# Two order edits around a layer's norms: w_out's last weight split behind a turn, SwiGLU 1's first post-norm multiply ahead of a weight split

## The chip, the cores and the metric

One core of a Trainium2 chip runs the whole layer. The metric is the device time of one execution in microseconds (us). Five engines work side by side, each through a queue of its own: PE (TensorE, matmuls; its weight loads are shown apart as PEld), DVE (VectorE), ACT (ScalarE), POOL (GpSimd) and SP (SyncE, which only issues transfers). An instruction waits for others through semaphores. About 0.2% of the time, 1.46 us here, is what a measurement of this kernel can tell from no change.

## The reference

A decoder layer on 256 tokens of width 1024, in fp32: a SwiGLU block (hidden width 2816), a mixer with a state-space branch and an attention branch, and a second SwiGLU block. Each is wrapped in RMS norms. Cut to what the change touches:

```
h = h + 0.5 * rmsnorm(swiglu(rmsnorm(h, ffn1_pre_g), ...), ffn1_post_g)
u = rmsnorm(h, mix_pre_g)
z, xbc, dt_raw, q, k, v, gate_logits = split(u @ w_in)
...
merged = gates[:, :, 0] * y_ssd + gates[:, :, 1] * y_att
h = h + rmsnorm(merged @ w_out, mix_post_g)
h = h + 0.5 * rmsnorm(swiglu(rmsnorm(h, ffn2_pre_g), ...), ffn2_post_g)
```

## The kernel before

**Splits.** Every fp32 product is made of three faster matmuls. An operand x is split into hi, a rounded copy of x (a cast on ACT), and lo = x - hi (a subtraction on DVE, which therefore follows the cast). PE then sums hi*hi, lo*hi and hi*lo. This holds for weights and activations alike. A weight chunk of 1 MB comes by DMA into one of three `raw` buffers, and `split_steps` (L256 to L275) splits it in two halves: cast `whi`, subtraction `wlo`, each 128 x 1024. Where the second lo part is done, the raw buffer is given back and the next load is issued on SP. Most products run over the two blocks of 128 tokens (block 0, block 1) and, on the output side, over two halves of 512 columns.

**Quads.** For some weights four 256-row chunks are combined as in Strassen's and Winograd's scheme (class `Quad`): seven products of sums replace eight. `Quad.split(p)` (L127 to L139) makes the hi and lo of piece p; the sums themselves (`wt`) are formed on DVE one or two pieces ahead. For w_out the pieces come in the order 1, 2, 6, 5, 3, 7, 4 (`MIXED`), and the two plain chunks of the lower half of w_out lie between 7 and 4 in the list of units. Piece 4's sum is formed together with piece 7's, at the split of piece 3, and at that point the raw buffers of the quad are given back. Its split thus issues no transfer.

**Who sets the order.** In the stages concerned only PE's order is written out by hand (`own_order(PE)`); it runs in the order of the program text. ACT, DVE and SP are ordered by the framework's planner. It takes for each engine the first instruction in the text that is ready when the engine comes free, by estimated times, and each engine's queue is then fixed: on the chip an instruction waits in its queue for its semaphores, and what stands behind it waits too. Buffers of one pool (`k4`, 29 of 4 KB a partition, hold most hi and lo parts) are handed out in the order of the text. `behind(m, "lo")` (L237 to L240) adds an edge of pure order to a DVE instruction: the planner must not place it ahead of the instruction noted in `normed["lo"]`. Such an edge carries no semaphore.

**w_out (`mm_mixed`, from L764).** The merged activations come as blocks (half of the columns, block of tokens). Both blocks of the first half are turned (transposed on PE into `pmg`, then split into `mh`, ml by `split`, L331 to L333, called in `turn_merged`) before `mm_mixed` begins. The two of the second half are turned inside it, one behind piece 6 and one behind piece 5, by `turn_next`. Line 793, `split_to(taken[0] + 9)`, puts the splits of all nine units into the text ahead of piece 1, the last of them piece 4. PE's order is: piece 1, 2, 6, first turn (block 0), piece 5, second turn (block 1), `plain(0, 0, 0)`, which is the first work that reads the turned second half of block 0, piece 3, further plain products, piece 7, block 1's plain products, piece 4. The post-norm of block 0 follows its last plain products: an add (L1728), a multiply by the gain (L617), a sum of squares on ACT (L518), the root on POOL (L523, L524), and h (L657).

**SwiGLU 1's end (`mm_n`, from L664).** The last three chunk pairs of the down product are held: PE runs block 0's first half of columns, then its second half, then block 1's. After each half, `half` adds the parts of the quads' bank to the accumulator (L1015) and calls `norm_half` (L607 to L617): a sum of squares on ACT (`jp`), for the first half a small add `ep` on DVE (L614), and the multiply by the gain into `og` (L617). `norm_end` (L648 to L657) makes the reciprocal root on ACT (`rp`) and h on DVE. Behind the call `ready(0)` (L714) the text splits the first chunk of the weights of V, the next product; of the four V chunks, the last has its parts held behind norm instructions of block 1. V's product (`Norm.products`, tile `pn_mx`, L394) runs over the four chunks for block 0, with the chunks' lo parts last.

Of the kernel before, what the change touches and what calls it, by code (L numbers as in the profile page):

```python
# [55 lines left out]
def tile_hybrid_layer(ctx: ExitStack, tc: tile.TileContext, x, ffn1_pre_g, ffn1_w_gate, ffn1_w_up,  # L56
# [25 lines left out]
    def pj(name):  # L82

        return ps.tile([P, 512], F32, tag="pj", name=name, bufs=3)
# [149 lines left out]
    normed = {"lo": None, "cast": None}  # L234
# [7 lines left out]
    taken = [0]  # L242
# [13 lines left out]
    def split_steps():  # L256


        i, _ = units[len(splits)]
        load_to(i + 1)  # L260
        r, shape = raws[i], chunks[i][1]
        nj = shape[1] // 2
        his, los = [], []
        splits.append((his, los))
        for q in range(2):
            hi = k4([P, nj, shape[2]], f"whi{i}{q}", F32R)
            lo = k4([P, nj, shape[2]], f"wlo{i}{q}", F32R)
            his.append(hi)
            los.append(lo)
            js = slice(q * nj, (q + 1) * nj)  # L270
            last_cast[0] = behind(nc.scalar.copy(hi, r[:, js, :]), "cast").ins  # L271
            m = nc.vector.tensor_sub(lo, r[:, js, :], hi.bitcast(F32))  # L272
            last_wlo[0] = behind(m, "lo").ins
            yield
        raws[i] = None  # L275
        load_to(i + 1 + RAW_BUFS)
# [23 lines left out]
    def split_to(n):  # L300

        while len(splits) < min(n, len(units)):
            of, p = units[len(splits)]
            if p is not None:
                splits.append(of.split(p))
                continue
            for _ in split_steps():
                pass

    def ahead_of(i, n):  # L310

        n *= 4
        while n > 0 and i < len(units):
            n -= 4 if units[i][1] is None else 1
            i += 1
        return i

    def take(ahead=AHEAD):

        i = taken[0]  # L320
        taken[0] += 1
        split_to(ahead_of(i, ahead))
        (of, p), w = units[i], splits[i]
        splits[i] = None
        if p is not None:
            return w
        his, los = w
        nj = chunks[of][1][1] // 2
        return (lambda j: his[j // nj][:, j % nj, :], lambda j: los[j // nj][:, j % nj, :])
# [334 lines left out]
    def mm_n(acc, acts, ready, turned, begun=lambda: None, pairs=None, begin=True, taken_all=lambda: None, norms=None,  # L664
             half=lambda b, q: None, quarters=(), tail=None):

        pairs = pairs or range(len(acts) // 2)
        n = len(pairs)
        held = []

        def one(i, w, parts, late=True, others=True, cs=slice(0, 512), to=None):


            wh, wl = w
            for kt in range(2):  # L680
                ah, al = acts[2 * pairs[i] + kt]
                for b, qs in parts:
                    ts = slice(b * P, (b + 1) * P)
                    for x_, w_ in ((ah, wh), (al, wh), (ah, wl)):
                        if not (late if kt == 1 and w_ is wl else others):
                            continue
                        for q in qs:
                            nc.tensor.matmul(acc[b][q][:, cs] if to is None else to, x_[:, ts],  # L688
                                             w_(kt)[:, halves[q]][:, cs],
                                             start=to is not None and kt == 0 and x_ is ah and w_ is wh or  # L690
                                             begin and i == 0 and kt == 0 and x_ is ah and w_ is wh,
                                             stop=i == (n - 2 if quarters and b and q and to is None else n - 1)
                                             and kt == 1 and w_ is wl)
                if i == 0:
                    begun()

        for i in range(n):
            w = take(min(n - i, AHEAD))
            if i < n - TAIL:
                one(i, w, ((0, (0, 1)), (1, (0, 1))))  # L700
            else:
                held.append((i, w))
        taken_all()
        own_order(PE)
        for q in range(2):
            for i, w in held:

                one(i, w, ((0, (q,)),), late=not norms or q == 1 or i < n - 1)
                if norms and q == 1 and i == n - TAIL:
                    one(*held[-1], ((0, (0,)),), others=False)  # L710
                    half(0, 0)
            if not norms or q == 1:
                half(0, q)
        ready(0)  # L714
        split_to(ahead_of(taken[0], AHEAD - 2))
        if norms:
            normed["lo"] = norms[0]["h"]
        split_to(ahead_of(taken[0], AHEAD - 1))
        for q in range(2):
            for i, w in held:  # L720
                if q == 1 and i == n - TAIL + (1 if norms else 0):
                    turned()
                if quarters and q == 1 and i == n - 1:
                    for cs, to in zip(quarters, tail):
                        one(i, w, ((1, (q,)),), cs=cs, to=to)
                else:
                    one(i, w, ((1, (q,)),))
            half(1, q)
        if not norms:
            split_to(ahead_of(taken[0], AHEAD))  # L730
        ready(1)
        if norms:
            if len(splits) < len(units):
                steps = split_steps()
                normed["lo"] = norms[1]["mul"]
                next(steps)
                normed.update(lo=norms[1]["h"], cast=norms[1]["exp"])
                for _ in steps:
                    pass
            normed.update(unit_done)  # L740
# [23 lines left out]
    def mm_mixed(acts, sums, turn_next, half, done, turned):  # L764


        at = {1: "a", 6: "a", 7: "a", 4: "a", 2: "b", 5: "d", 3: "d"}
        banks = {"a": pj("acc_mxa")}
        begun = set()
        sh, sl = sums  # L770
        p1, u2, p5, c4 = (k2([P, 512], f"{n}_mx") for n in ("p1", "u2", "p5", "c4"))

        def mm(o, x_, w_, stop):
            nc.tensor.matmul(banks[o], x_, w_, start=o not in begun, stop=stop, skip_group_check=True)
            begun.add(o)

        def piece(p, w):
            o, (wh, wl) = at[p], w
            if o not in banks:
                banks[o] = bg([P, 512], f"acc_mx{o}")  # L780
            for kt in range(2):
                ah, al = of_piece(p, kt, acts[:4], sh, sl)
                for x_, w_ in ((ah, wh), (al, wh), (ah, wl)):
                    mm(o, x_, w_(kt), kt == 1 and w_ is wl and p in (1, 5, 6, 7))

        def plain(b, q, i):
            o, (wh, wl) = (("b", "d"), ("a", "e"))[b][q], ws[i]
            for kt in range(2):
                ah, al = (x_[:, b * P:(b + 1) * P] for x_ in acts[4 + 2 * i + kt])
                for x_, w_ in ((ah, wh), (al, wh), (ah, wl)):  # L790
                    mm(o, x_, w_(kt)[:, halves[q]], i == 1 and kt == 1 and w_ is wl)

        split_to(taken[0] + 9)
        piece(1, take(0))
        nc.scalar.copy(p1, banks["a"])
        piece(2, take(0))
        piece(6, take(0))
        nc.scalar.copy(u2, banks["a"])
        turn_next()
        piece(5, take(0))  # L800
        nc.scalar.copy(p5, banks["d"])
        turn_next()
        w3, w7 = take(0), take(0)
        ws = [take(0) for _ in range(2)]
        w4 = take(0)
        plain(0, 0, 0)
        piece(3, w3)
        split_to(taken[0] + 1)
        steps = split_steps()
        next(steps)  # L810
        plain(0, 1, 0)
        plain(0, 0, 1)
        half(0, 0, banks["b"], p1)
        plain(0, 1, 1)
        half(0, 1, banks["d"], u2)
        normed["lo"] = done(0)
        for _ in steps:
            pass
        piece(7, w7)
        nc.vector.tensor_tensor(c4, banks["a"], p5, ALU.add)  # L820
        banks["e"] = pj("acc_mxe")
        plain(1, 1, 0)
        plain(1, 1, 1)
        half(1, 1, banks["e"], c4)
        turned()
        piece(4, w4)
        for i in range(2):
            plain(1, 0, i)
        half(1, 0, banks["a"], None)
        normed["lo"] = done(1)  # L830
# [946 lines left out]
```

## Time and profile before

| what | us |
|---|---|
| median of 3 runs | 730.65 |
| lowest and highest | 729.85, 730.78 |
| the profiled execution's own time | 731.11 |
| its span, first to last instruction | 729.4 |
| PE busy in the span | 720.5 |
| DVE busy | 621.8 |
| ACT busy | 478.8 |

The profiled execution took 1.71 us more than its span; this lies around the span. A row of the timeline gives start, duration, engine, source line, operation and output <- inputs, and in brackets the time the engine stood idle before the row with what released it. Rows that follow each other closely are merged ("x2"). Matmuls overlap in a pipeline: one of 512 columns is shown with 0.39 us though the next starts 0.23 us after it, so a delay of PE is read from start to start. ACT and DVE rows also overlap a little: two lo parts of 1.22 us take 2.35 us together.

### The profile page before, as it was taken

Reading aid. Unit: us, or ns where it says so; the run is one execution under the profiler, and the core shown is the slowest. Engines: PE = TensorE matmul, PEld = TensorE weight load, DVE = VectorE, ACT = ScalarE, POOL = GpSimd, SP = SyncE. Lnnn points to the kernel's source line nnn. Section 1 sums busy time; section 2 is a strip of 40 time slices with the busy share of each in tenths; the row PEclk is TensorE's granted clock in tenths of the full one; section 3 lists DMA queues with packets and bytes.
Section 4 is the critical chain, followed back from the end, with each engine's and each line's share of the span. In section 5 each row is a group of like instructions: output and inputs, shape, how many; then the busy total and the mean of one; then the engine's idle time right before and its main releaser. Section 6 shows DMA issues by size and latency. Waiting matters only on the chain.

```text
span 729.4 us, 10595 instructions
## 1 busy us (share of the span) xinstructions
PE 720.5 (99%) x4019; PEld 619.4 (85%) x4019; DVE 621.8 (85%) x950; ACT 478.8 (66%) x816; POOL 30.9 (4%) x63
## 2 busy tenths in 40 slices
PE   9999999999999999999999999999999999999996
PEld 7888888888778889999888788888788888888885
DVE  6978788999979999777996998789776878789996
ACT  5667566666867676969965577784654756576562
POOL 4300000000200000000000000000011000000000
PEclk9999999999999999999999999999999999999999
DMA  8884655567573557666564664464543655754451
GB/s 298 234 263 152 220 163 184 174 230 259 181 232 118 180 167 231 215 181 212 154 224 146 205 225 135 153 234 170 181 138 116 231 182 165 231 191 156 180 194 58
DMA packets 94451, 137.93 MB, mean 189 GB/s; under 512 B 2668, under 2 KB 68800, under 8 KB 94400
## 3 DMA queue, kind: packets, MB, share of 16 engines
q1 hardware_dynamic: 91728, 129.51, 53.8%
q0 software_dynamic: 2368, 7.22, 3.2%
q8 instruction: 31, 0.51, 0.3%
q10 hardware_dynamic: 304, 0.53, 0.2%
q14 instruction: 20, 0.16, 0.1%
HBM read 136.17 MB, written 1.08 MB: 188 GB/s over the span
## 4 chain that ended last, share of the span: by engine, by line
PE 88%; DVE 5%; ACT 2%; DMA 2%; issue 2%; SPq 0%; DVEq 0%; ACTq 0%
PE pup_f L353 14%; PE pg_f L353 14%; PE pxs L353 6%; PE pws L394 6%; PE pgt L394 6%; PE acc_f2p L842 5%; PE pbc L353 3%; PE pk L353 3%; PE pq L353 3%; PE pn_f L394 3%; PE pwd L394 3%; PE pn_f L410 3%; PE pn_mx L394 2%; PE acc_f2p L688 2%; PE pz L345 2%
## 5 line engine op out<-in xcount | busy, mean ns | idle before, releaser
L272 DVE TENSOR_TENSOR wlo<-raw,whi 128x1024 fp32r<-128x1024 f32 x212 | 252.7, 1221 | 18.7 <-ACT whi L271 18.2
L271 ACT CAST whi<-raw 128x1024 fp32r<-128x1024 f32 x212 | 214.4, 1048 | 14.0 <-DMA raw<-in_w_in_dram 5.8
L353 PE MATMUL pg_f<-u_f,whi 128*128 128x512 f32 x288 | 69.1, 390 | 0.0
L353 PE MATMUL pup_f<-u_f,whi 128*128 128x512 f32 x288 | 68.7, 391 | 0.0
L353 PEld LDWEIGHTS pg_f<-u_f,whi 128*128 128x128 f32 x288 | 53.9, 188 | 11.2
L353 PEld LDWEIGHTS pup_f<-u_f,whi 128*128 128x128 f32 x288 | 52.9, 188 | 10.2
L131 ACT CAST wqh<-wt 128x1024 fp32r<-128x1024 f32 x24 | 25.2, 1054 | 23.3 <-DVE wt L123 21.9
L353 PEld LDWEIGHTS pg_f<-u_f,wlo 128*128 128x128 f32 x288 | 36.9, 191 | 1.4
L353 PE MATMUL pup_f<-u_f,wlo 128*128 128x256 f32 x288 | 37.5, 283 | 0.0
L353 PE MATMUL pg_f<-u_f,wlo 128*128 128x256 f32 x288 | 37.4, 283 | 0.0
L359 ACT COPY su_f<-pup_f 128x256 f32<-128x256 f32 x36 | 13.2, 372 | 35.9 <-PE pup_f L353 35.9
L353 PEld LDWEIGHTS pup_f<-u_f,wlo 128*128 128x128 f32 x288 | 35.9, 192 | 0.0
L360 DVE TENSOR_TENSOR su_f<-pup_f,su_f 128x256 f32<-128x256 f32 x36 | 15.2, 422 | 24.0 <-ACT su_f L359 23.9
L394 PE MATMUL pgt<-whi,u_mx 128*128 128x512 f32 x128 | 33.1, 393 | 0.0
L343 PE MATMUL pz<-u_mx,whi 128*128 128x256 f32 x128 | 31.6, 284 | 0.0
L342 PE MATMUL pz<-u_mx,whi 128*128 128x256 f32 x128 | 31.6, 284 | 0.0
L353 PE MATMUL pxs<-u_mx,whi 128*128 128x512 f32 x128 | 29.9, 390 | 0.0
L137 DVE TENSOR_TENSOR wql<-wt,wqh 128x1024 fp32r<-128x1024 f32 x24 | 29.1, 1220 | 0.2
L137 DVE TENSOR_TENSOR wql<-raw,wqh 128x1024 fp32r<-128x1024 f32 x21 | 25.5, 1220 | 3.4 <-ACT wqh L131 3.4
L394 PEld LDWEIGHTS pgt<-whi,u_mx 128*128 128x128 f32 x128 | 23.6, 188 | 5.3 <-issue 0.7
L353 PEld LDWEIGHTS pxs<-u_mx,whi 128*128 128x128 f32 x128 | 23.8, 188 | 4.8
L332 ACT CAST gh_f<-sg_f 128x512 fp32r<-128x512 f32 x18 | 11.2, 621 | 23.2 <-DVE sg_f L995 20.3
(487 smaller groups left out, 1607.5 us busy)
## 6 DMA issues: line engine op xcount, KB each, us to landing
raw<-in_w_in_dram SPq DMA_DIRECT2D x40, 1024.0 KB, 5.2
raw<-in_ffn_w_down_dram SPq DMA_DIRECT2D x22, 1024.0 KB, 4.8
raw<-in_ffn_w_gate_dram SPq DMA_DIRECT2D x20, 1024.0 KB, 5.5
raw<-in_ffn_w_up_dram SPq DMA_DIRECT2D x20, 1024.0 KB, 5.2
raw<-in_ssd_w_branch_dram SPq DMA_DIRECT2D x8, 1024.0 KB, 4.9
acb<-acd POOLq DMA_DIRECT2D x8, 512.0 KB, 4.4
raw<-in_da_w_branch_dram SPq DMA_DIRECT2D x4, 1024.0 KB, 5.0
raw<-in_w_out_dram SPq DMA_DIRECT2D x4, 1024.0 KB, 6.2
```

The costliest lines, as they stand in the source:

```text
L131: nc.scalar.copy(hi, src)
L137: nc.vector.tensor_sub(lo, src, hi.bitcast(F32))
L271: last_cast[0] = behind(nc.scalar.copy(hi, r[:, js, :]), "cast").ins
L272: m = nc.vector.tensor_sub(lo, r[:, js, :], hi.bitcast(F32))
L342: nc.tensor.matmul(acc[m], wh(j)[:, cs], ah(k0 + j), start=first and j == ks[0], stop=False)
L343: nc.tensor.matmul(acc[m], wh(j)[:, cs], al(k0 + j), start=False, stop=False)
L345: nc.tensor.matmul(acc[m], wl(j)[:, cs], ah(k0 + j), start=False, stop=last and j == ks[-1])
L353: nc.tensor.matmul(to, w_(j)[:, m * P:(m + 1) * P], x_(j), start=first and j == 0, stop=not first and j == KD - 1, skip_group_check=True)
L360: nc.vector.tensor_tensor(dst, acc[:, :T], dst, ALU.add)
L394: nc.tensor.matmul(acc, a(k0 + j), b(j), start=first and i == 0, stop=last and i == 11)
L410: nc.tensor.matmul(accs[b], x_(k0 + j), w_(j), start=first and j == 0 and w_ is wh and x_ is acts[b][0], stop=last and j == 3 and w_ is wl)
L842: nc.tensor.matmul(bank[p], x_, w_, start=p not in begun, stop=last and p in (1, 5, 6, 7))
```

## The change

Three lines change. In `mm_n` the multiply of block 0's first half is noted as the instruction behind which "lo" instructions must stay: this holds for the lo parts of V's first chunk (up to L715, the next unit) and for the adds of `half(0, 1)`. `mm_n` serves both SwiGLU blocks. In `mm_mixed` the list is split up to the second plain chunk only (eight units), and the ninth, piece 4, is split behind the first `turn_next()`.

```diff
@@ -709,6 +709,7 @@
                 if norms and q == 1 and i == n - TAIL:
                     one(*held[-1], ((0, (0,)),), others=False)
                     half(0, 0)
+                    normed["lo"] = norms[0]["mul"]
             if not norms or q == 1:
                 half(0, q)
         ready(0)
@@ -790,13 +791,14 @@
-        split_to(taken[0] + 9)
+        split_to(taken[0] + 8)
         piece(1, take(0))
         nc.scalar.copy(p1, banks["a"])
         piece(2, take(0))
         piece(6, take(0))
         nc.scalar.copy(u2, banks["a"])
         turn_next()
+        split_to(taken[0] + 6)
         piece(5, take(0))
         nc.scalar.copy(p5, banks["d"])
         turn_next()
```

## The prediction

> **What bounds the kernel now.** I read the page first (engines, chain), then the waits of PE, then the timelines of PE, ACT and DVE around those waits.
>
> ```profile
> PE 720.5 (99%) x4019; PEld 619.4 (85%) x4019; DVE 621.8 (85%) x950; ACT 478.8 (66%) x816; POOL 30.9 (4%) x63
> ...
> PE 88%; DVE 5%; ACT 2%; DMA 2%; issue 2%; SPq 0%; DVEq 0%; ACTq 0%
> ```
> ```profile
> PE acc_mxb L774 <- DVE ml L333: 0.9, 1, 0.9
> PE pn_mx L394 <- DVE wlo L272: 0.5, 1, 0.5
> ```
>
> PE is the bound: it is busy all but 8.9 us, and the chain of waits lies on it for 88%. Nothing can be won but PE's own stalls. Behind the start its waits show just the two above: in w_out for a turned activation, in V for a weight's lo part. Each edit stands ahead of one of them on DVE. PE in w_out, some rows left out:
>
> ```profile
> 523.99 0.60 PE L1689 MATMUL pmg<-ident,gt 128*128 128x128 f32 x4
> 524.35 0.48 PE L774 MATMUL acc_mxd<-wqh,sh 128*128 128x512 f32 x1
> ...
> 525.13 0.40 PE L774 MATMUL acc_mxd<-wqh,sh 128*128 128x512 f32 x1
> ...
> 525.82 0.60 PE L1689 MATMUL pmg<-ident,gt 128*128 128x128 f32 x4
> 526.26 0.50 PE L774 MATMUL acc_mxb<-whi,mh 128*128 128x512 f32 x1
> 527.64 0.50 PE L774 MATMUL acc_mxb<-whi,ml 128*128 128x512 f32 x1 [0.88 <-DVE ml L333]
> ...
> 528.21 0.40 PE L774 MATMUL acc_mxb<-whi,mh 128*128 128x512 f32 x1
> ```
>
> The wait costs more than its 0.88 us, because the bracket starts where the pipelined matmul before it ends. Start to start is the honest measure. From the first turn to the fourth matmul behind it: 525.13 - 523.99 = 1.14. From the second turn: 528.21 - 525.82 = 2.39. The same work, so the stall is **1.25 us**.
>
> A rule to weigh against the bracket: the Trainium skill ("Trainium Kernel Development and Optimization", Performance Expectations) calls matmul busy time a bad measure of how far a kernel is from its limit, because matmuls are pipelined, and names the busy share of the weight loads instead. Two windows of 10 us (PE, then PEld, DVE, ACT, POOL, clock, DMA):
>
> ```profile
> 520.00:530.00 10.00, 9.12 (x44) 7.28 (x43) 9.56 (x13) 7.35 (x11) 0.00 (x0) 1.00 0.65 209
> 530.00:540.00 10.00, 10.00 (x49) 8.34 (x49) 7.84 (x11) 4.42 (x10) 0.88 (x2) 1.00 0.33 107
> ```
>
> Loads fall from 8.34 to 7.28, which is 10 x 1.06 / 8.34 = 1.27 us of lost time. Matmul busy would give 0.88. The rule's reading and start to start agree; with 0.88 the sum below would be 0.37 smaller.
>
> **Part one, w_out.** Why ml is late, ACT first, then DVE:
>
> ```profile
> 524.67 1.05 ACT L131 CAST wqh<-wt_mx 128x1024 fp32r<-128x1024 f32 x1
> 525.62 0.59 ACT L332 CAST mh<-pmg 128x512 fp32r<-128x512 f32 x1
> ```
> ```profile
> 522.96 2.36 DVE L272 TENSOR_TENSOR wlo<-raw,whi 128x1024 fp32r<-128x1024 f32 x2
> 525.76 1.23 DVE L137 TENSOR_TENSOR wql<-wt_mx,wqh 128x1024 fp32r<-128x1024 f32 x1 [0.44 <-ACT wqh L131]
> 526.90 1.28 DVE L333 TENSOR_TENSOR ml<-pmg,mh 128x512 fp32r<-128x512 f32 x2
> 528.16 3.50 DVE L272 TENSOR_TENSOR wlo<-raw,whi 128x1024 fp32r<-128x1024 f32 x3
> 533.19 0.69 DVE L1728 TENSOR_TENSOR p_mx<-acc_mxb,p_mx 128x512 f32<-128x512 f32 x1 [1.53 <-PE acc_mxb L774]
> ```
>
> Piece 4's cast and subtraction stand ahead of the first turn's on both engines, though the piece is the last that PE reads. The change moves two instructions, no transfer: the quad's raw buffers were given back earlier. With them behind the turn, the turn's transposes end at 523.99 + 0.60 = 524.59 and mh takes wqh's place at 524.67, until 525.26. DVE ends its lo parts at 525.32; ml of block 0 runs from about 525.35 to 526.05 (half of the merged pair, some 0.69). PE wants mh at 526.18 (0.36 behind 525.82, as at the first turn) and ml one matmul later, not before 526.4. Both are there, ml with 0.3 to spare, so all 1.25 is gained.
>
> What is queued behind: wqh next on ACT, 525.2 to 526.2, and then the copy of piece 5's product and mh of block 1, within 0.1 of where they are. wql on DVE ends at about 527.5, ml of block 1 at 528.1, the lo parts of SwiGLU 2 follow at 528.1 as before. Block 1 and piece 4 are read after 534, so this cost lies under PE's work. DVE's cover is thinner than it was. It is free at 528.1 + 3.50 = 531.6, and p_mx's add, 1.25 earlier, falls due at 531.94: 0.3 spare where 1.53 stood. The four pool buffers only change partners. I take 1.25. Bounds: 0 if the planner leaves the order as it was, 1.25 at most since the stall then is gone.
>
> **Part two, SwiGLU 1.** PE in V:
>
> ```profile
> 194.80 0.61 PE L394 MATMUL pn_mx<-wlo,u_mx 128*128 128x512 f32 x2
> 195.87 0.72 PE L394 MATMUL pn_mx<-wlo,u_mx 128*128 128x512 f32 x2 [0.46 <-DVE wlo L272]
> 196.44 1.09 PE L394 MATMUL pn_mx<-whi,u_mx 128*128 128x512 f32 x4
> ```
>
> Four matmuls took 196.44 - 194.80 = 1.64 us. A row of four lasts 1.09 and a row of two 0.61, so a step is 0.24 and four are 0.96: a stall of **0.68**. The awaited lo part started at 194.60 and DVE worked with hardly a gap from 179.44 on. DVE, then ACT:
>
> ```profile
> 177.30 0.68 DVE L1015 TENSOR_TENSOR p_f<-acc_f1p,p_f 128x512 f32<-128x512 f32 x1
> 179.44 1.23 DVE L272 TENSOR_TENSOR wlo<-raw,whi 128x1024 fp32r<-128x1024 f32 x1 [1.46 <-ACT whi L271]
> 180.59 0.69 DVE L617 TENSOR_TENSOR og_f<-p_f,pg_f 128x512 f32<-128x512 f32 x1
> 181.19 0.14 DVE L614 TENSOR_SCALAR ep_f<-sp_f 128x1 f32<-128x1 f32 x1
> 181.25 0.68 DVE L1015 TENSOR_TENSOR u_f<-acc_f1p,u_f 128x512 f32<-128x512 f32 x1
> ...
> 183.59 1.41 DVE L657 SCALAR_TENSOR_TENSOR h<-og_f,rp_f,h 128x512 f32<-128x512 f32 x2
> 194.60 1.21 DVE L272 TENSOR_TENSOR wlo<-raw,whi 128x1024 fp32r<-128x1024 f32 x1
> ```
> ```profile
> 178.36 2.00 ACT L271 CAST whi<-raw 128x1024 fp32r<-128x1024 f32 x2 [5.82 <-DMA raw<-in_w_in_dram]
> 180.26 0.62 ACT L518 ACTIVATE jp_f<-p_f 128x512 f32<-128x512 f32 x1
> 180.79 0.19 ACT L518 ACTIVATION_READ_ACCUMULATOR jp_f<-p_f 128x1 f32 x1
> ...
> 181.97 0.63 ACT L518 ACTIVATE jp_f<-u_f 128x512 f32<-128x512 f32 x1
> ...
> 183.05 0.20 ACT L427 ACTIVATE rp_f<-rp_f 128x1 f32<-128x1 f32 x1
> ```
>
> At 177.98 DVE took V's lo part, whose chunk had not landed, and idled 1.46 with the multiply ready behind it. Ahead of the lo part the multiply fits into that gap (178.0 to 178.7), and its 0.60 (181.19 - 180.59) falls off DVE's row. How much reaches V depends on ACT. **(a)** ACT keeps its order: ep needs the read at 180.98, so the add starts at 181.07 instead of 181.25: 0.18. **(b)** Casts and lo parts alternate in the pool's order of buffers, so V's second cast can be placed only once its first lo part is; that is now later in the plan, and the square jp of p_f, ready since 177.98, goes ahead of it. Then jp runs at 179.31 to 180.03, the second cast ends at 181.08, and the two have changed places, so what follows on ACT stays put. The add starts at 180.64, the second lo part at 181.24, the second multiply ends near 183.0, and h waits for rp at 183.25: 183.28 instead of 183.59, 0.31. **(c)** All 0.60, or the stall's 0.68, if the later square moves up too. From h on the row is dense and PE gets the same shift at 195.87. Against it: the add is barred by the same edge and could be placed ahead of the lo part with the square still late; then DVE idles until 181.0, h comes about 1.0 late and V with it. So the bounds are -1.0 and +0.68.
>
> Whether casts and lo parts alternate shows on ACT in w_out, at the second plain chunk's second cast:
>
> ```profile
> 521.47 0.59 ACT L795 COPY p_mx<-acc_mxa 128x512 f32<-128x512 f32 x1 [1.76 <-PE acc_mxa L774]
> 521.95 1.05 ACT L271 CAST whi<-raw 128x1024 fp32r<-128x1024 f32 x1
> ```
>
> It comes behind the copy, though ACT idled 1.76 ahead of that with the chunk long loaded; the chunk's first lo part is the one at 522.96 on DVE, late behind the merge. So the alternation holds there, and I take (b), **0.31**.
>
> In SwiGLU 2 the new edge costs nothing: no splits are left, and the add there stands behind the multiply already, waiting for PE. If that cover were gone, the edge still carries no semaphore.
>
> **Sum.** 1.25 + 0.31 = 1.56. The profiled execution took 731.11 (span 729.4 and 1.71 around it): 729.55 after. The median of the runs lies 0.46 below it: 730.65 - 1.56 = **729.1**.
>
> **Rivals.**
> - *Only w_out pays*: ACT's order holds, or PE meets V's lo part as late as before: 1.25 to 1.43, 729.3. For it: the swap on ACT in (b) is the planner's choice by its own times, which no row shows. Against it: the multiply leaves DVE's full row in any case.
> - *V's stall goes whole*: 1.25 + 0.68: 728.7. It needs the square of u_f ahead of a cast, which the order of before has behind it.
> - *Given back in w_out's norm*: one more lo part (1.17, a third of 3.50) ahead of p_mx's add makes it 0.9 late, h and the turn behind it too: 730.0. For it: 0.3 spare. Against it: that part's cast is fourth and must come first.
> - *The edit in w_out changes nothing*, the planner putting piece 4 first again since it is ready: 730.3. Against it: mh's buffers come first in the text.
> - *Slower*: the planner's order tips over far from the edits, in the state-space branch. There ACT's exponentials E feed PE without slack:
>
> ```profile
> 293.73 2.00 ACT L271 CAST whi<-raw 128x1024 fp32r<-128x1024 f32 x2
> ...
> 303.98 0.96 DVE L1360 TENSOR_TENSOR E<-E,cbm 128x768 f32<-128x768 f32 x1 [0.73 <-ACT E L427]
> ```
> ```profile
> 304.99 2.82 PE L1370 MATMUL py<-E,X 128*64 128x256 f32 x32
> ```
>
> PE's py starts 0.05 behind the last E. Two more casts ahead of it cost 2.00 for each of the four groups in which it happens; one group gives 731.1, two give 733.1, and from one on the gain is gone. For it: ACT's order is re-planned behind the first edit. Against it: PE bounds that stretch, so everything there moves together.
>
> **How the numbers follow.** Forecast 0.52, w_out alone 0.14, whole stall 0.13, given back 0.07, no change in w_out 0.05, slower 0.09. What can be told from no change is 0.2%, 1.46 us: faster means below 729.19. The forecast lies 0.1 below that line, so with a scatter of some 0.35 between runs 0.33 of its 0.52 counts as faster, with 0.13 of the whole stall and 0.04 of w_out alone: 0.50. Slower by 0.2% is the last case, 0.09; the rest, 0.41, is within. The range, 728.3 to 730.6, takes the cases from 728.7 to 730.3 with 0.3 to 0.4 for scatter and leaves out the slower case. The forecast's own is 728.7 to 729.5.
>
> **What would show it.** Right: no wait of PE for ml; mh ahead of the cast of piece 4 on ACT; from the second turn to the fourth matmul 1.14; the multiply og_f before 179; jp of p_f before V's second cast; PE's wait in V shorter by 0.3, not gone. Wrong: a wait of PE at the turn behind w_out, DVE reaching p_mx's add with no idle time before it, py waiting longer for E, or h of block 0 later against the add of p_f than now (6.29).

## The result, and the profile after

| | before | after |
|---|---|---|
| median on the same chip, 22 runs each (us) | 730.26 | 728.78 |
| lowest and highest | 729.40, 730.88 | 728.42, 730.06 |
| the profiled execution's own time | 731.11 | 728.73 |
| its span | 729.4 | 727.0 |

The ratio is 0.9982 [0.9975, 0.9988]: 1.3 us gained, with an interval of 0.9 to 1.8. The medians differ by 1.48. The 1.46 us that a measurement of this kernel can tell from no change lies between the two: the interval is clear of zero, and the gain about as large as that line. The forecast was 729.1, its own range 728.7 to 729.5.

The page of the changed kernel, engines and chain of waits:

```profile
PE 719.0 (99%) x4019; PEld 618.8 (85%) x4019; DVE 621.4 (85%) x950; ACT 479.0 (66%) x816; POOL 32.2 (4%) x63
...
PE 96%; ACT 2%; DMA 1%; DVE 1%; issue 0%; SPq 0%; DVEq 0%; ACTq 0%
```

The waits of PE (engine, tile and line, what it waited for: us in all, times, longest):

```profile
PE warm L487 <- DVE zeros L467: 1.1, 1, 1.1
PE pn_f L410 <- DVE whi L289: 0.7, 1, 0.7
```

Both waits for DVE that stood in w_out and V are gone; what is left lies at the kernel's start. The chain lies on PE for 96% instead of 88%, but that says little of the change: a second profile of the kernel before, further down, has 96% too.

w_out on PE, first turn, the fourth matmul behind it, second turn, and the matmuls behind that:

```profile
522.89 0.60 PE L1691 MATMUL pmg<-ident,gt 128*128 128x128 f32 x4
...
524.03 0.40 PE L775 MATMUL acc_mxd<-wqh,sh 128*128 128x512 f32 x1
...
524.72 0.60 PE L1691 MATMUL pmg<-ident,gt 128*128 128x128 f32 x4
525.07 0.48 PE L775 MATMUL acc_mxb<-whi,mh 128*128 128x512 f32 x1
525.39 0.39 PE L775 MATMUL acc_mxb<-whi,ml 128*128 128x512 f32 x1
525.62 0.40 PE L775 MATMUL acc_mxb<-wlo,mh 128*128 128x512 f32 x1
525.86 0.39 PE L775 MATMUL acc_mxb<-whi,mh 128*128 128x512 f32 x1
```

From the second turn to the fourth matmul it is 525.86 - 524.72 = 1.14, as behind the first (524.03 - 522.89). Before it was 2.39: the 1.25 us is gained to the hundredth. The profiles of the experiments below agree: the stretch takes 2.38 to 2.41 in all six with w_out's old order, that of before among them, and 1.13 to 1.14 in all eight with the new one. ACT and DVE show how:

```profile
523.57 0.59 ACT L332 CAST mh<-pmg 128x512 fp32r<-128x512 f32 x1
524.05 1.06 ACT L131 CAST wqh<-wt_mx 128x1024 fp32r<-128x1024 f32 x1
```
```profile
524.20 0.69 DVE L333 TENSOR_TENSOR ml<-pmg,mh 128x512 fp32r<-128x512 f32 x1
525.14 1.23 DVE L137 TENSOR_TENSOR wql<-wt_mx,wqh 128x1024 fp32r<-128x1024 f32 x1 [0.25 <-ACT wqh L131]
...
530.83 0.69 DVE L1730 TENSOR_TENSOR p_mx<-acc_mxb,p_mx 128x512 f32<-128x512 f32 x1 [0.26 <-PE acc_mxb L775]
```

The cast mh stands ahead of piece 4's cast wqh, ml runs at 524.20, and piece 4's subtraction comes behind it. The idle time ahead of p_mx's add shrinks from 1.53 to 0.26.

The Trainium skill ("Trainium Kernel Development and Optimization", Performance Expectations) would have the weight loads' busy share watched instead of the matmuls'. The 10 us that hold w_out's turns show it (PE, PEld, DVE, ACT, POOL, clock, DMA): 8.29 us of loads where 7.28 stood, so the rule reads this gain where matmul busy, 9.12 and then 10.00, shows 0.88 of it.

```profile
518.90:528.90 10.00, 10.00 (x50) 8.29 (x49) 9.64 (x13) 7.35 (x11) 0.00 (x0) 1.00 0.66 211
```

SwiGLU 1's end, DVE and then ACT:

```profile
177.10 0.68 DVE L1017 TENSOR_TENSOR p_f<-acc_f1p,p_f 128x512 f32<-128x512 f32 x1
177.82 0.69 DVE L617 TENSOR_TENSOR og_f<-p_f,pg_f 128x512 f32<-128x512 f32 x1
178.58 1.23 DVE L272 TENSOR_TENSOR wlo<-raw,whi 128x1024 fp32r<-128x1024 f32 x1
179.72 0.14 DVE L614 TENSOR_SCALAR ep_f<-sp_f 128x1 f32<-128x1 f32 x1
179.79 0.68 DVE L1017 TENSOR_TENSOR u_f<-acc_f1p,u_f 128x512 f32<-128x512 f32 x1
...
182.41 1.41 DVE L657 SCALAR_TENSOR_TENSOR h<-og_f,rp_f,h 128x512 f32<-128x512 f32 x2 [0.21 <-ACT rp_f L427]
```
```profile
177.50 1.05 ACT L271 CAST whi<-raw 128x1024 fp32r<-128x1024 f32 x1 [5.01 <-DMA raw<-in_w_in_dram]
178.45 0.62 ACT L518 ACTIVATE jp_f<-p_f 128x512 f32<-128x512 f32 x1
...
179.07 2.12 ACT L271 CAST whi<-raw 128x1024 fp32r<-128x1024 f32 x2
...
182.17 0.20 ACT L427 ACTIVATE rp_f<-rp_f 128x1 f32<-128x1 f32 x1
```

The multiply og_f stands ahead of V's first lo part, the square jp of p_f ahead of V's second cast, and h waits for rp. From V's first cast to h it is 182.41 - 177.50 = 4.91, where the kernel before has 183.59 - 178.36 = 5.23: 0.32 less, with 0.31 forecast. But PE in V does not wait at all:

```profile
194.52 1.07 PE L394 MATMUL pn_mx<-wlo,u_mx 128*128 128x512 f32 x4
195.43 1.07 PE L394 MATMUL pn_mx<-whi,u_mx 128*128 128x512 f32 x4
196.34 1.03 PE L532 MATMUL pu_mx<-ident,un_mx 128*128 128x128 f32 x8
```

Four lo matmuls take 195.43 - 194.52 = 0.91 from start to start. The 1.64 of before therefore held a stall of 0.73, and all of it is gone, not 0.3 of it. More than the edit is at work. V's first cast began 8.08 behind the issue of its load before (170.28 to 178.36) and 7.42 behind it after (170.08 to 177.50):

```profile
170.28 4.91 SPq L253 DMA_DIRECT2D raw<-in_w_in_dram  x3
```
```profile
170.08 11.91 SPq L253 DMA_DIRECT2D raw<-in_w_in_dram  x4
```

The chunk landed 0.66 sooner behind its issue, and the change touches neither this load nor one ahead of it. Whether the stall went by the change or by chance was left to the experiments.

The lead of the execution after over that before grows from 0.20 at that issue to 1.03 at the turn behind V's first block (197.37 and 196.34), 1.10 at w_out's first turn, 2.35 at w_out's fourth matmul (528.21 and 525.86) and 2.37 at the last h. So 1.25 came in w_out, 0.83 between V's load and V's end, and 0.2 was there before any edit acts. SwiGLU 2, which the new edge also serves, lost nothing: from w_out's fourth matmul to the last h it is 196.82 before and 196.80 after.

### The profile page after: what moved, and what is told of

Same layout as the page of the kernel before. It is cut to its first block, busy times and chain, and to the rows that moved or that the text cites. A ratio compares the mean times of both kernels' runs of the same rounds, so it can differ in the third digit from the quotient of the medians.

```text
span 727.0 us, 10595 instructions
## 1 busy us (share of the span) xinstructions
PE 719.0 (99%) x4019; PEld 618.8 (85%) x4019; DVE 621.4 (85%) x950; ACT 479.0 (66%) x816; POOL 32.2 (4%) x63
## 4 chain that ended last, share of the span: by engine, by line
PE 96%; ACT 2%; DMA 1%; DVE 1%; issue 0%; SPq 0%; DVEq 0%; ACTq 0%
PE pup_f L353 14%; PE pg_f L353 14%; PE pxs L353 6%; PE pws L394 6%; PE pgt L394 6%; PE acc_f2p L844 5%; PE acc_f1p L844 5%; PE pbc L353 3%; PE pk L353 3%; PE pq L353 3%; PE pn_mx L394 3%; PE pn_f L394 3%; PE pwd L394 3%; PE pn_f L410 3%; PE acc_f1p L688 2%; PE acc_f2p L688 2%
```

## The experiments

The runs of the kernel before have their median at 729.92, 729.93, 729.98 and 729.69 in the four groups that follow.

**Each edit alone.** Only the two lines in `mm_mixed`, and only the line in `mm_n`:

```diff
# wout_only
-        split_to(taken[0] + 9)
+        split_to(taken[0] + 8)
...
         turn_next()
+        split_to(taken[0] + 6)
```

> Only the w_out edit; SwiGLU 1 as before. Theory (the two edits act apart, w_out's stall was 1.25 us and goes whole): 1.25 us under the kernel before, ratio 0.9983; from the second turn to the fourth matmul 1.14; V keeps its wait, of a size set by when V's first chunk lands. Rival (most of the gain comes from SwiGLU 1, whose stall went whole in the profile of the changed kernel): about 0.6 us under before, ratio 0.9992.

```diff
# norm_only
                     half(0, 0)
+                    normed["lo"] = norms[0]["mul"]
```

> Only the SwiGLU 1 edit; w_out as before. Theory (the multiply moves into DVE's gap, h comes 4.9 us behind the start of V's first cast instead of 5.2, the rest of what the profile showed was an earlier landing): 0 to 0.35 us under before, ratio 0.9995 to 1.0; h 4.9 behind the first cast; w_out keeps its 0.88 wait. Rival (the edit took the whole stall): 0.7 to 0.85 under before, ratio 0.9989, and no wait in V whatever the landing.

w_out's edit alone: 728.91, ratio 0.9987 [0.9978, 0.9996], 0.95 us gained (0.3 to 1.6). From the second turn to the fourth matmul its trace has 525.83 - 524.69 = 1.14:

```profile
524.69 0.60 PE L1690 MATMUL pmg<-ident,gt 128*128 128x128 f32 x4
...
525.83 0.39 PE L774 MATMUL acc_mxb<-whi,mh 128*128 128x512 f32 x1
```

SwiGLU 1's edit alone: 730.00, ratio 0.9998 [0.9989, 1.0007], nothing that can be told; in its trace PE waits for ml as before:

```profile
PE acc_mxb L775 <- DVE ml L333: 0.9, 1, 0.9
```

The surprise is V in the first of the two. It has SwiGLU 1's old order, and yet no wait of PE in V. Its chunk landed early:

```profile
175.37 2.00 ACT L271 CAST whi<-raw 128x1024 fp32r<-128x1024 f32 x2 [3.24 <-DMA raw<-in_w_in_dram]
```
```profile
176.90 0.68 DVE L1016 TENSOR_TENSOR p_f<-acc_f1p,p_f 128x512 f32<-128x512 f32 x1
177.49 1.22 DVE L272 TENSOR_TENSOR wlo<-raw,whi 128x1024 fp32r<-128x1024 f32 x1
...
181.62 1.41 DVE L657 SCALAR_TENSOR_TENSOR h<-og_f,rp_f,h 128x512 f32<-128x512 f32 x2
```

The first cast began at 175.37, only 5.50 behind the issue at 169.87; DVE took the lo part directly behind the add of p_f and h came 4.72 behind that add, against 6.29 in the profile of before. The stall of 0.73 was no property of the order alone.

**The chunk in two transfers.** The changed kernel with V's first chunk loaded by halves, so that its first cast need not wait for the whole:

```diff
-            nj = shape[1] // 4 if i == 0 else shape[1] // 2 if i < 4 else shape[1]
+            nj = shape[1] // 4 if i == 0 else shape[1] // 2 if i < 4 or i == 33 else shape[1]
```

> The changed kernel with V's first chunk loaded in two transfers of half the size, so that its first half can land earlier. Theory (what is left of V's stall hangs on the landing): V's first cast starts sooner than 7.4 us behind the issue, no wait in V in the profile, time 0 to 0.3 us under the changed kernel, 1.5 to 1.8 under before. Rival (landing does not matter once the multiply is ahead): same time as the changed kernel; a loss of up to 0.3 if the two smaller transfers slow the neighbours.

729.08, ratio 0.9987 [0.9978, 0.9995]: no faster than the change itself. The first cast began 3.86 behind the issue, 3.16 ahead of the add of p_f, and h still 4.86 behind that add. Once the chunk is there ahead of the add, an earlier landing brings nothing.

**The cover in w_out's norm taken away.** The prediction's rival "given back" forced: one more lo part, the second half of a weight chunk's split, ahead of the add of p_mx (in `mm_mixed`, `next(steps, None)` once more behind `next(steps)`).

> The changed kernel with one more lo part of SwiGLU 2 ahead of the post-norm add in w_out, so that DVE's spare time before it (0.26 in the profile of the changed kernel) is overdrawn by about 0.9. As the prediction priced it: the add, h and the turn behind it 0.9 late, 0.9 us slower than the changed kernel, 0.6 under before. Rival (h hangs on the second half's add, which waits for PE until 1.3 us later, so the late first add is caught up): the second add within 0.2 of where it is, no wait of PE, time within 0.2 us of the changed kernel.

728.93, ratio 0.9985 [0.9976, 0.9994], not to be told from the change. DVE in that run:

```profile
527.65 4.63 DVE L272 TENSOR_TENSOR wlo<-raw,whi 128x1024 fp32r<-128x1024 f32 x4
532.20 0.69 DVE L1731 TENSOR_TENSOR p_mx<-acc_mxb,p_mx 128x512 f32<-128x512 f32 x1
532.80 0.68 DVE L1731 TENSOR_TENSOR u_mx<-acc_mxd,u_mx 128x512 f32<-128x512 f32 x1
...
535.54 1.42 DVE L657 SCALAR_TENSOR_TENSOR h<-og_mxp,rp_mxp,h 128x512 f32<-128x512 f32 x2 [0.86 <-POOL rp_mxp L524]
```

Four lo parts instead of three stand ahead of the add. It comes 532.20 - 525.30 = 6.90 behind the second turn of PE, where the changed kernel has 530.83 - 524.72 = 6.11: 0.79 late, near the 0.9 of the prediction. But h is only 0.17 later (10.24 against 10.07 behind the turn, 534.79 in the changed kernel): the add of the second half now follows at once, and h waits for rp of POOL in both. PE's next product begins 16.53 behind the turn (541.83), where the changed kernel has 16.32 (541.04 - 524.72): 0.21, not 0.9.

**Repeats.** The changed kernel and the kernel before once more, unchanged, in one group.

> The changed kernel once more, for a second profile and a second interval. Theory: ratio 0.998; w_out 1.14 from the second turn to the fourth matmul; h 4.9 behind the start of V's first cast; PE waits in V only if that cast starts more than about 7.7 us behind the issue of its load. Rival (V's stall is gone for good): no wait in V at any landing.

> The kernel before once more, unchanged, for the landing of V's first chunk in another execution. Theory: h 5.2 behind the first cast in any case; PE's wait in V moves with the landing one to one and is gone if the cast starts under about 7.4 us behind the issue. Rival: the wait in V is 0.5 again though the landing moves. Ratio 1.

The change again: 728.53, ratio 0.9982 [0.9973, 0.9991]; before: 729.98, ratio 1.0001 [0.9991, 1.0010]. The kernel before shows V's stall at another size, PE and then DVE:

```profile
194.87 1.24 PE L394 MATMUL pn_mx<-wlo,u_mx 128*128 128x512 f32 x4
195.94 1.10 PE L394 MATMUL pn_mx<-whi,u_mx 128*128 128x512 f32 x4
```
```profile
177.40 0.68 DVE L1015 TENSOR_TENSOR p_f<-acc_f1p,p_f 128x512 f32<-128x512 f32 x1
178.94 1.23 DVE L272 TENSOR_TENSOR wlo<-raw,whi 128x1024 fp32r<-128x1024 f32 x1 [0.87 <-ACT whi L271]
```

1.07 instead of 0.91, a stall of 0.16 where the same program had 0.73. Its first cast began 7.48 behind the issue instead of 8.08.

**Which of ACT's orders carries the 0.32.** In the first program the changed kernel's square of p_f is held behind V's second cast (ACT's order of before); in the second the kernel before has the square ahead of that cast, and the multiply stays behind V's first lo part. One edge of order each, where that cast is issued (`squares[0]` is the square of p_f, unit 33 V's first chunk):

```diff
# cast_first (in the changed kernel)
+            if i == 33 and q == 1:
+                tc.add_manual_dep(squares[0], last_cast[0].name, order, reason="the cast first")
# square_first (in the kernel before)
+            if i == 33 and q == 1:
+                tc.add_manual_dep(last_cast[0], squares[0].name, order, reason="the square first")
```

> The changed kernel with the old order on ACT: V's second cast held ahead of the square of p_f. By step (b) of the prediction, where ACT's swap carries the gain: h back to about 5.05 behind the first cast (0.18 gained). Rival (the multiply's move alone carries it, up to the root rp, which ACT reaches at the same time either way): h 4.9 behind the first cast, as in the changed kernel.

> The kernel before with ACT's swap alone: the square of p_f ahead of V's second cast, the multiply still behind V's first lo part. Theory (the multiply's 0.6 on DVE is the cause): h 5.2 behind the first cast, as before. Rival (the swap on ACT gains by itself): h 4.9 to 5.0.

One run each: 728.72 and 729.65. The first program, ACT and then DVE:

```profile
176.96 2.00 ACT L272 CAST whi<-raw 128x1024 fp32r<-128x1024 f32 x2 [4.80 <-DMA raw<-in_w_in_dram]
178.87 0.62 ACT L521 ACTIVATE jp_f<-p_f 128x512 f32<-128x512 f32 x1
...
181.63 0.20 ACT L430 ACTIVATE rp_f<-rp_f 128x1 f32<-128x1 f32 x1
```
```profile
179.35 0.68 DVE L1020 TENSOR_TENSOR u_f<-acc_f1p,u_f 128x512 f32<-128x512 f32 x1
179.95 0.14 DVE L617 TENSOR_SCALAR ep_f<-sp_f 128x1 f32<-128x1 f32 x1
...
181.87 1.41 DVE L660 SCALAR_TENSOR_TENSOR h<-og_f,rp_f,h 128x512 f32<-128x512 f32 x2
```

Both casts stand ahead of the square, and h still comes 181.87 - 176.96 = 4.91 behind the first cast. So in this order the 0.32 does not hang on ACT's swap. The planner put ep behind the add of u_f here, so the prediction's variant (a), with ep ahead of it, was not seen; whether the swap is needed there stays open. The second program says nothing on this: its chunk landed early, and h came 4.73 behind the add of p_f, as in the other early executions.

**The chunk made late.** To cause the late landing rather than wait for it, 0.5 MB (a lo part, written to a scratch that nobody reads) goes ahead of V's first load on SP's queue, in the kernel before and in the changed one:

```diff
+            if i == 33:
+                lo = splits[-1][1][-1]
+                nc.sync.dma_start(dram.tile(list(lo.shape), F32, tag="late", name="late"), lo.bitcast(F32))
             for j in range(0, shape[1], nj):
```

> The kernel before with one more transfer of 0.5 MB (a lo part written to a scratch in DRAM, read by nobody) on SP's queue directly ahead of V's first load, released by the same lo part; every other queue is the same. Theory: V's stall is set by when V's first chunk lands. Loads follow each other at 1 MB in some 2.3 to 3.1 us, so the chunk lands 1.2 to 1.6 later than it would; over the runs so far V's first cast started between 1.66 ahead of and 1.06 behind the add of p_f, so here between 0.3 ahead and 2.6 behind. By the traces of the kernel before, h starts 5.23 behind that cast, and PE stalls in V for what h is later than some 5.55 behind the add: a stall between 0 and 2.3, most likely near 0.9; the median time 0.4 to 1.0 above before. Rival: the stall comes from DVE's full row, as the prediction costed it, and the landing matters little: a stall no longer than 0.7, the time as before.

> The changed kernel with the same extra transfer. Theory: h starts 4.91 behind V's first cast, 0.32 sooner than in the kernel before with the same transfer, so PE's stall in V is 0.3 shorter at the same landing, and with the 1.25 of w_out the time is some 1.5 below that of the kernel before with the extra transfer, where between the kernels without it SwiGLU 1's edit gave nothing that can be told. Rival: the edit's 0.32 does not reach PE even where the chunk is late: a difference of 1.0 to 1.25, and PE's stall the same at the same landing.

730.38, ratio 1.0005 [0.9996, 1.0014], and 729.40, 0.9992 [0.9983, 1.0001]. Inconclusive in time: the first is 0.4 above the kernel before, the second 0.6 to 0.9 above the changed kernel's two medians from other groups, and their difference of 0.98 fits either side. The landing that was to be caused did not come: in the profiled executions the first cast began 6.54 and 6.66 behind the issue of V's load, no later than without the extra transfer, and within 0.1 of the add's start. There was no stall in either, where some 0.9 had been expected in the kernel before. h stood 5.23 behind the cast in the one (181.96 - 176.73) and 4.86 in the other (181.54 - 176.68), as the theory has it.

**More of it.** The same part twice on POOL's queue (`nc.gpsimd.dma_start`) beside V's first load.

> The kernel before with 1 MB more on POOL's queue beside V's first load (one lo part written twice to a scratch in DRAM, read by nobody), released by the lo part that releases that load; the order of the other engines and of SP is the same. Theory: the two share the DMA engines, V's first chunk lands 1 to 2.5 later than it would, h starts 5.23 behind the first cast, and PE stalls in V for what h is later than 5.5 behind the add of p_f: 0.3 to 3 in the profile, the time 0.5 to 2 above before. Rival: the stall comes from DVE's full row and not from the landing: no stall over 0.7, the time as before.

> The changed kernel with the same 1 MB more. Theory: where the chunk is late, h starts 4.91 behind the first cast, 0.32 sooner than in the kernel before, and PE's stall is what h is later than 5.5 behind the add: 0.3 shorter at the same landing; the time 1.25 + 0.3 below that of the kernel before with the same transfers, if the landings are alike, which their scatter of 1 or more may hide. Rival: the edit's 0.32 does not reach PE: the stall counted from the first cast is the same as in the kernel before.

734.05 and 733.09, ratios 1.0047 [1.0034, 1.0060] and 1.0043 [1.0029, 1.0057]. These missed their aim: V's first chunk was not late (its cast began 6.58 and 6.60 behind the issue). Late was the gain vector pg_f, 0.5 MB on POOL's own queue, which og_f reads: its issue now stood behind the two added ones, which waited for the lo part until 169.93. In the changed kernel with these transfers, POOL and DVE:

```profile
170.99 0.53 POOL L665 DMA_DIRECT2D pg_f<-in_ffn_post_g_dram  x1
```
```profile
176.68 0.68 DVE L1021 TENSOR_TENSOR p_f<-acc_f1p,p_f 128x512 f32<-128x512 f32 x1
182.77 0.69 DVE L621 TENSOR_TENSOR og_f<-p_f,pg_f 128x512 f32<-128x512 f32 x1 [5.41 <-DMA pg_f<-in_ffn_post_g_dram]
183.38 1.22 DVE L276 TENSOR_TENSOR wlo<-raw,whi 128x1024 fp32r<-128x1024 f32 x1
```

pg_f landed 11.7 behind its issue, og_f waited 5.41 for it, and V's first lo part, whose cast had run at 176.26, stood behind og_f. In the kernel before with these transfers the same lo part ran at 176.89, ahead of og_f, which waited here too:

```profile
181.40 0.69 DVE L621 TENSOR_TENSOR og_f<-p_f,pg_f 128x512 f32<-128x512 f32 x1 [3.28 <-DMA pg_f<-in_ffn_post_g_dram]
```

So h is late in both, and most of the lateness is not the edit's. From og_f to h it is 3.55 in the kernel before (h at 184.95) and 4.14 in the changed one (h at 186.91): by these two profiles the edit costs 0.59 behind a late gain vector. In the times the changed kernel is still the faster of the two, by 0.96 in the medians of five runs each, w_out's 1.25 included. So the edit has a condition of its own: the gain vector must be there when the add of p_f ends. In the changed kernel without these transfers pg_f is issued at 166.96 and lands 5.5 later, 5.4 ahead of og_f.

**What the runs show together.** c is V's first cast's start less the add of p_f's start; then h's start behind that cast and behind that add, and V's stall, which is the time of the four lo matmuls beyond 0.91. The two runs in which the gain vector was late are left out.

| run | order in SwiGLU 1 | c | h behind cast | h behind add | stall in V |
|---|---|---|---|---|---|
| before | old | 1.06 | 5.23 | 6.29 | 0.73 |
| before_again | old | 0.45 | 5.23 | 5.68 | 0.16 |
| late_before | old | -0.04 | 5.23 | 5.19 | 0 |
| square_first | old, square first | -0.49 | 5.22 | 4.73 | 0 |
| wout_only | old | -1.53 | 6.25 | 4.72 | 0 |
| after | new | 0.40 | 4.91 | 5.31 | 0 |
| late_after | new | 0.08 | 4.86 | 4.94 | 0 |
| cast_first | new, cast first | 0.07 | 4.91 | 4.98 | 0 |
| after_again | new | -0.61 | 5.47 | 4.86 | 0 |
| no_cover | new | -1.58 | 6.43 | 4.85 | 0 |
| norm_only | new | -1.66 | 6.51 | 4.85 | 0 |
| after_two_loads | new | -3.16 | 8.02 | 4.86 | 0 |

In the old order h follows the later of two: the cast by 5.23, the add by 4.72. In the new order it follows the cast by 4.91 (4.86 once) and the add by 4.85. PE stalls only where h is more than about 5.5 behind the add. So in the new order h gains 0.3 where the chunk is late and loses 0.13 where it is early, and with an early chunk PE feels nothing of either. The pair nearest in landing, before_again and after, shows that the edit reaches PE: c of 0.45 and 0.40, a stall of 0.16 and none, of which the landing itself explains 0.05. A later chunk under the new order, where the whole 0.3 should reach PE, was not seen. Three of these twelve executions have a c of 0.4 or more.

## Why the prediction was right, and where it was not

*The bound and w_out.* PE was the bound, and the start-to-start reading gave the stall's size: 1.25 forecast, 1.25 measured, 0.95 (0.3 to 1.6) in the times of w_out's edit alone. The order came out as forecast on both engines, and DVE's cover ahead of p_mx's add shrank to 0.26, with 0.3 forecast.

*SwiGLU 1.* The step that failed is the one that took V's stall for a fixed term of the kernel: "a stall of **0.68**", read from one execution. Its size there was 0.73, because four matmuls take 0.91 and not the 0.96 pieced together from row lengths; but in another execution of the same program it was 0.16, and three of the five executions in the old order, two of them with an edit near it, had none. So the prediction's own sign, PE's wait in V "shorter by 0.3, not gone", did not come. What decides is when V's first chunk lands. The edit's own price, from the first cast to h, was right (0.32 for 0.31), and by the table it reaches PE only behind a late chunk. An estimate of its mean, from the nine executions of the table without an altered or added transfer: at the landing of before the new order would put h 1.06 + 4.91 = 5.97 behind the add, a stall of 0.43 between the two measured (0.16 at 5.68, 0.73 at 6.29), a gain of 0.30; at that of before_again the whole 0.16; at that of after the old order would have had h at 5.63, a stall of some 0.11; in the other six nothing. That is 0.57 over nine, 0.06 us. That fits the edit alone, which gave nothing that can be told. Whether it adds 0 or 0.4 to the median is below what these runs resolve.

*What carries it.* Variant (b) gave the 0.31 to the swap on ACT. The swap came, as forecast from the alternation of casts and lo parts, but the one run without it does not need it: with the cast ahead of the square, and ep behind the add, h was just as early. In all three orders rp ends 4.87 to 4.89 behind the first cast (183.25 - 178.36, 182.37 - 177.50, 181.83 - 176.96). In the old order h was 0.34 later than rp because DVE was still at its row; with the multiply out of that row h meets rp.

*The sum.* 1.56 was forecast for the profiled execution and 2.38 came; the medians moved by 1.48, and the ratio makes it 1.3. That 1.56 lies near them is in part luck. 1.25 of it was earned in w_out; the other 0.31 was taken off a stall that is there in some executions only, 0.06 in the mean by the estimate above. The start was off the other way: 730.65, the median of three runs, lay 0.39 above that of the 22. So the forecast of 729.1 came out 0.3 above 728.78: 0.39 too high at the start, with 0.08 too much gain against the medians. The profiled execution of before, 731.11, lay above every one of the 22 runs of before. Its late chunk, worth 0.7, is a part of why.

*The rivals.* "Only w_out pays" is, for the typical execution, nearest to what the edits do one by one, though by neither of its two conditions: ACT's order did change, and mostly there is no stall to take. "V's stall goes whole" is what the profile after shows, by an earlier landing and the edit's 0.32 together (0.98, more than the 0.73), and not by the square that the prediction named. "Given back" had its lateness right (0.79 for 0.9) and its price wrong: 0.21 on PE, since the second half's add closes up and rp waits on POOL anyway. "Changes nothing" fell with the order on ACT. "Slower" did not come: the last E of the group at 303 waits 0.74 for ACT where it waited 0.73.

*What was not named.* The multiply that moves up reads pg_f, a transfer on POOL's queue. Its cover, 5.4 us here, should have stood in the working; with the queue crowded the move cost h some 0.6.

## What to carry to other kernels

A stall whose end is a transfer's landing is a draw, not a constant: compare at least two profiles of the same program before taking it for a term, and measure it against the landing. A stall that hangs on the order of instructions alone, as w_out's, can be read from one profile, from start to start: it came out the same within 0.03 in six. When an instruction moves up, list the transfers it reads too, with the time by which each has landed.

## What the runs showed of the hardware

The same 1 MB load, with the same work around it, landed 5.4 to 8.1 us behind its issue (the first cast's start; nine executions without an altered or added transfer). It goes with the rate of the transfers at that time: over the two us from 173 that is 245 GB/s at the latest landing (8.08), 287 to 337 at the five between (6.41 to 7.48), and 407, 385 and 394 at the three earliest (5.50, 5.45, 5.37). These two us in the kernel before and with w_out's edit alone (last two columns: busy share of the 16 DMA engines, GB/s):

```profile
173.00:175.00 2.00, 2.00 (x10) 1.68 (x9) 2.00 (x3) 0.00 (x0) 0.00 (x0) 1.00 0.89 245
```
```profile
173.00:175.00 2.00, 2.00 (x10) 1.66 (x9) 1.99 (x3) 0.00 (x0) 0.00 (x0) 1.00 1.05 407
```

The engines are busy in both. Why the rate differs, no run here shows. The Trainium skill ("DMA: Bandwidth & Descriptors", Anatomy of one DMA) fits a transfer from POOL's queue by 2.0 us and its bytes at 436 GB/s; as an estimate for 1 MB that is 4.4 us. By that V would never have stalled; the landings here, 5.4 at the least, differ from it, on SP's queue and with other loads in flight, and the measurement decides.

On DVE an instruction that reads the result of the one ahead starts later than one that does not: og_f 0.72 behind the add of p_f that it reads (177.10 to 177.82), the lo part in the same place 0.59 (176.90 to 177.49), both adds of 0.68. That is the 0.13 by which the new order has the longer row.
